# Bulk steps of a state-space scan: products moved from two engines to ScalarE, in a kernel that interleaves the scan with attention

## The chip, the cores and the metric

One core of a Trainium2 chip runs the whole program in one launch. The metric is the device time of that launch in microseconds (us); lower is better. The engines are named as the profile names them: PE is TensorE (matrix products), DVE is VectorE, ACT is ScalarE, POOL is GpSimd and SP is SyncE, which here only issues transfers.

## What is computed

The reference is a two-layer backbone over 1024 latent tokens and 256 context tokens of width 1024, in fp32. Layer 0 runs latent attention (8 heads) and a bidirectional S5 state-space layer side by side; layer 1 is a gated recurrence; each layer ends with a convolutional feed-forward part. Only layer 0's mixer is touched here:

```python
# attention, per head, over context + latent tokens
s = einsum('bqhd,bkhd->bhqk', q, k) * MLA_SCALE
p = softmax(s); att = einsum('bhqk,bkhd->bqhd', p, v)

# S5, 32 groups of 64 complex states, both directions
x = einsum('blgp,gnp->blgn', u, bb)            # re and im
s = associative_scan(s[t] = lb * s[t-1] + x[t])  # complex
y = Re(einsum('blgn,gpn->blgp', s, c)) + d * u  # gelu, gate
z = gelu(y); z = z * sigmoid(z @ w_glu)
out = concat([att, z]) @ w_out
```

## The kernel before

The program is written once as a stream of tile operations. The tile framework orders each engine's instructions when it builds the program, from priorities (the order in which they are written) and its own timeline; on the chip every engine then works through its own list in that fixed order. Where the text speaks of an order, it is this list.

**Attention** (`attention`, from L694). `qk(h)` makes the keys and queries of head h and `attend(h)` uses them, one head behind; `merge` interleaves the steps of `attend(h)`, `qk(h + 1)`, the S5 half-passes and the adaLN products (tile `pada`, L257). All fp32 products of attention are made from rounded high and low parts (`mm3`, L100 to L105: three products; `split`, L108 to L114: a copy to the high part on ACT and a subtraction for the low one). For each block of 512 or 256 queries `attend` goes over 10 (or 2) key tiles: scores in `pS` by `mm3`, the exponential `p` on ACT (L821), its rounded part `ph` on ACT and its rest `pl` on DVE or POOL in turn (L111, L114), and three products into `po` (L826 to L828). The tiles `p`, `ph` and `pl` have two places each.

The softmax needs a maximum per query. `qk` computes rounded scores once more (L793), reduces them on DVE (`mx`, L796, and `mm`, L801 or L803), turns the column of maxima into a row with one fp32 product per 128 queries against the identity (`pm`, L806) and stores the row as row 96 of the queries in high and low parts (L807: the copy on ACT, the subtraction on DVE). Scores then come out with the maximum subtracted.

**S5** (`S5Half.run`, from L867). Twice, for 16 groups each ("half 0" and "half 1"): the inputs `U` are loaded and multiplied into the state tile `H` (`pV`, L889, evicted on ACT at L892), for both directions d. Then comes a scan in three parts over 160 slots of 8 tokens: a bulk pass up over two levels, a sequential scan over every fourth slot on POOL (38 steps of three operations, L931 to L934), and a bulk pass down over two levels. The outputs `pY` (L950, L953) follow, with a gelu on ACT and DVE (L954 to L959), and go to DRAM as `Zd`, from where the gate (`zs`, `pglu`) reads them after attention.

A bulk step is a complex multiply-add on strided slots: two operations. Direction 0 runs on DVE, direction 1 on POOL:

```python
e.tensor_tensor(t, Mh[...].to_broadcast([128, n, 2, 16]), at(src, [[0, 2], [161, 16]]), op=OP.mult)   # L908
for b in range(2):
    e.tensor_tensor(o, o, t[:, :, :, 8 * b:8 * b + 8], op=OP.add)                                     # L912
```

Each product instruction covers up to 16 (DVE) or 20 (POOL) slots. There are four bulk stages in the program: half 0 up, half 0 down, half 1 up, half 1 down. In this text they are stages A, B, C and D. In the trace they lie at about 306 to 343, 404 to 460, 673 to 714 and 795 to 852 us.

Of the kernel before, what the change touches and what calls it, by code (L numbers as in the profile page):

```python
# [11 lines left out]
R = mybir.dt.float32r  # L12
I32 = mybir.dt.int32
AF = mybir.ActivationFunctionType
OP = mybir.AluOpType
# [5 lines left out]
T = SEQ + CTX  # L21
# [672 lines left out]
def attention(k, A):  # L694
    nc = k.nc
    P = Pool(k, "att")
# [4 lines left out]
    for b in range(2):  # L701
        split(nc, KT[b][0][64:96, :], KT[b][1][64:96, :], k.rope[64:96, :], elo="v")
        nc.vector.tensor_copy(KT[b][0][96:97, :], k.ones[96:97, 0:1].to_broadcast([1, T]))
        nc.vector.tensor_copy(KT[b][1][96:97, :], k.zero[96:97, 0:1].to_broadcast([1, T]))
        nc.gpsimd.tensor_copy(Vt[b][0][:, :, 64:128], k.ones[:, 0:1].unsqueeze(1).to_broadcast([128, 10, 64]))
    wkv = A["mla_w_ukv"][0].rearrange("(a p) (h m) -> p a h m", p=128, m=128)
    wuq = A["mla_w_uq"][0].rearrange("(a p) m -> p a m", p=128)
# [1 line left out]
    gk = k.cols[:, k.at["mla_kv_norm", 0]:][:, 0:2]  # L709
    vd = k.tc.dram_tile([T, 512], F, name="vd")  # L710
    S5 = S5Half(k, A)


    vp = Pool(k, "vp")
# [21 lines left out]
    def qk(h):  # L736
# [30 lines left out]
        for s, e in BLK:  # L767
            n = e - s
            ps = bank(k, "pq", "C")
            with behind(k, k.pace):  # L770
                for a in range(3):
                    mm3(nc, ps[:, :n], [w[:, a * 128:a * 128 + 128] for w in wq], [x[a][:, s:e] for x in cq], a == 0, a == 2)
            t = W([128, 512], tag="tq", bufs=2)
            nc.vector.tensor_tensor(t[0:64, :n], ps[64:128, :n], k.rqk[64:128, s:e], op=OP.mult)
            nc.vector.tensor_tensor(t[64:96, :n], ps[0:32, :n], k.rope[0:32, s:e], op=OP.mult)
            if s < SEQ:
                x = W([128, 512], tag="rc")
                nc.vector.tensor_tensor(x[64:96, :n], ps[32:64, :n], k.rope[32:64, s:e], op=OP.mult)
                nc.vector.tensor_tensor(t[64:96, :n], t[64:96, :n], x[64:96, :n], op=OP.add)
            split(nc, q[0][0:96, s:e], q[1][0:96, s:e], t[0:96, :n], elo="v")  # L780
            yield 1

            kb = BLK if s < SEQ else BLK[2:]
            mx = W([128, 4, 3], tag="mx", bufs=2)
            mm_ = W([128, 4], tag="mm", bufs=2)
            nt = n // 128
            jobs = [(j, (i,), ks, ke) for i in range(nt) for j, (ks, ke) in enumerate(kb) if ke < T]
            jobs += [(len(kb) - 1, (i, i + 1), SEQ, T) for i in range(0, nt, 2)]
            for x, (j, tiles, ks, ke) in enumerate(jobs):
                ps = bank(k, "pS", "C")  # L790
                for i, t in enumerate(tiles):
                    with behind(k, k.pace):
                        nc.tensor.matmul(ps[:, i * 256:i * 256 + ke - ks], lhsT=q[0][0:96, s + t * 128:s + t * 128 + 128],  # L793
                                         rhs=kk_[0][0:96, ks:ke], start=True, stop=True)
                t, m = tiles[0], len(tiles)
                nc.vector.tensor_reduce(mx[:, t:t + m, j:j + 1], ps[:].rearrange("p (m x) -> p m x", m=m),  # L796
                                        axis=AX.X, op=OP.max, negate=True)
                if x % 3 == 2 or x == len(jobs) - 1:
                    yield 1
            if len(kb) > 1:  # L800
                nc.vector.tensor_reduce(mm_[:, :nt], mx[:, :nt, :len(kb)], axis=AX.X, op=OP.min)  # L801
            else:
                nc.vector.tensor_copy(mm_[:, :nt], mx[:, :nt, 0])  # L803
            pm = bank(k, "pm", "C")
            for i in range(nt):
                nc.tensor.matmul(pm[96:97, i * 128:i * 128 + 128], lhsT=mm_[:, i:i + 1], rhs=k.ident[:], start=True, stop=True)  # L806
            split(nc, q[0][96:97, s:e], q[1][96:97, s:e], pm[96:97, :n], elo="v")  # L807
            yield 1

    def attend(h):  # L810
        b = h % 2
        q, kk_, v = QT[b], KT[b], Vt[b]
        for s, e in BLK:
            n = e - s
            po = bank(k, "po", "B")
            tiles = list(range(10)) if s < SEQ else [8, 9]
            for i, t in enumerate(tiles):
                ps = bank(k, "pS", "A")
                k.pace = mm3(nc, ps[:, :n], [x[0:97, t * 128:t * 128 + 128] for x in kk_], [x[0:97, s:e] for x in q], True, True)
                p = PP([128, 512], tag="p", bufs=2)  # L820
                nc.scalar.activation(p[:, :n], ps[:, :n], AF.Exp, scale=SCALE)  # L821
                ph = PP([128, 512], R, tag="ph", bufs=2)
                pl = PP([128, 512], R, tag="pl", bufs=2)
                split(nc, ph[:, :n], pl[:, :n], p[:, :n], ehi="a", elo="p" if i % 2 else "v")
                st, sp = i == 0, i == len(tiles) - 1
                nc.tensor.matmul(po[:, :n], lhsT=v[0][:, t], rhs=ph[:, :n], start=st, stop=False)  # L826
                nc.tensor.matmul(po[0:64, :n], lhsT=v[1][:, t], rhs=ph[:, :n], start=False, stop=False, skip_group_check=True)
                nc.tensor.matmul(po[:, :n], lhsT=v[0][:, t], rhs=pl[:, :n], start=False, stop=sp)  # L828
                yield 1


            o = AO([128, 512], tag="ao")
            nc.scalar.activation(o[0:65, :n], po[0:65, :n], AF.Copy)
            nc.sync.dma_start(out=k.attd[64 * h:64 * h + 64, s:e], in_=o[0:64, :n])
            k.last_sum = nc.sync.dma_start(out=k.atts[h:h + 1, s:e], in_=o[64:65, :n])
            yield 1
# [19 lines left out]
class S5Half:  # L856
# [11 lines left out]
    def run(self):  # L868
        k, nc, P = self.k, self.k.nc, self.P
        E = nc.gpsimd  # L870
        for hh in range(2):
# [26 lines left out]
            def bulk(i, up, d):  # L898


                h = 1 << i
                e, tag, m = ((nc.vector, "RO", 16), (E, "Tm", 20))[d]
                src, dst = ((h, 2 * h), (h, 0))[d] if up else ((0, h), (2 * h, h))[d]
                for j in range(0, 80 // h, m):
                    n = min(m, 80 // h - j)
                    t = P([128, m, 2, 16], tag=tag, bufs=2 - d)[:, :n]
                    at = lambda s0, dims: raw(H, s0 + 2 * h * j + 16 * 161 * d, [[2 * h, n]] + dims)
                    e.tensor_tensor(t, Mh[:, i, d].rearrange("p a b q -> p a (b q)").unsqueeze(1)  # L908
                                    .to_broadcast([128, n, 2, 16]), at(src, [[0, 2], [161, 16]]), op=OP.mult)
                    o = at(dst, [[8 * 161, 2], [161, 8]])  # L910
                    for b in range(2):
                        e.tensor_tensor(o, o, t[:, :, :, 8 * b:8 * b + 8], op=OP.add)  # L912
                    yield 1

            def both(levels, up):
# [752 lines left out]
```

## Time and profile before

| what | value |
|---|---|
| median of 3 runs | 3792.78 us (3787.41 to 3795.8) |
| time of the profiled execution | 3789.94 us |
| its span on the core | 3788.1 us |
| mean granted clock of TensorE | 0.966 of full speed |
| busy share of the span: PE, DVE, ACT, POOL | 95%, 55%, 29%, 31% |
| attention and S5 | about 240 to 930 us of the span |

The granted clock is the share of TensorE's full 2.4 GHz that it was given; its two levels are 2.4 and 1.2 GHz. A busy share close to 100% at a clock of 1.00 means that TensorE sets the pace of a stretch; a lower share or a lower clock means that something else does.

### The profile page before, as it was taken

Reading aid. Unit: us, or ns where it says so; the run is one execution under the profiler, and the core shown is the slowest. Engines: PE = TensorE matmul, PEld = TensorE weight load, DVE = VectorE, ACT = ScalarE, POOL = GpSimd, SP = SyncE. Lnnn points to the kernel's source line nnn. Section 1 sums busy time; section 2 is a strip of 40 time slices with the busy share of each in tenths; the row PEclk is TensorE's granted clock in tenths of the full one; section 3 lists DMA queues with packets and bytes.
Section 4 is the critical chain, followed back from the end, with each engine's and each line's share of the span. In section 5 each row is a group of like instructions: output and inputs, shape, how many; then the busy total and the mean of one; then the engine's idle time right before and its main releaser. Section 6 shows DMA issues by size and latency. Waiting matters only on the chain.

```text
span 3788.1 us, 47489 instructions
## 1 busy us (share of the span) xinstructions
PE 3588.2 (95%) x19081; PEld 2910.3 (77%) x19081; DVE 2101.3 (55%) x3294; ACT 1082.7 (29%) x1798; POOL 1178.5 (31%) x1089
## 2 busy tenths in 40 slices
PE   6987899888999999999998999999998999999997
PEld 3764566556788888888887889898987888888885
DVE  7736855784555444444447655565664744545445
ACT  2323445445332121111113322222221511212123
POOL 3627823782442211111114411111122622212122
PEclk9997999988999999999999999999998999999998
DMA  7462345304201111111110210101022111111111
GB/s 243 120 169 73 110 120 141 98 23 146 84 23 34 40 44 40 39 34 34 40 34 29 78 34 29 40 29 40 29 67 89 45 45 45 52 44 51 45 45 45
DMA packets 294301, 243.05 MB, mean 64 GB/s; under 512 B 41214, under 2 KB 255576, under 8 KB 293056
## 3 DMA queue, kind: packets, MB, share of 16 engines
q1 hardware_dynamic: 289152, 227.32, 20.4%
q10 hardware_dynamic: 4928, 12.69, 1.0%
q8 instruction: 150, 2.46, 0.3%
q14 instruction: 71, 0.58, 0.0%
HBM read 203.79 MB, written 38.28 MB: 64 GB/s over the span
## 4 chain that ended last, share of the span: by engine, by line
PE 82%; DVE 7%; POOL 2%; DMA 2%; issue 1%; ACT 1%; SPq 0%; ACTq 0%; POOLq 0%; DVEq 0%
PE pa L105 5%; PE po L103 5%; PE pa L103 5%; PE pa L104 5%; PE po L104 5%; PE po L105 5%; PE pg L103 5%; PE pg L105 5%; PE pg L104 5%; PE ph L104 3%; PE ph L105 3%; PE ph L103 3%; PE pA L1419 3%; PE pmix L103 2%; PE pmix L104 2%; PE pmix L105 2%
## 5 line engine op out<-in xcount | busy, mean ns | idle before, releaser
L114 POOL TENSOR_TENSOR w<-ws,w 128x1024 fp32r<-128x1024 f32 (+1 forms) x205 | 501.1, 2449 | 1570.7 <-ACT w L111 1424.4
L1051 DVE SCALAR_TENSOR_TENSOR acc<-po,mod,acc 128x512 f32<-128x512 f32 (+1 forms) x456 | 309.3, 679 | 559.3 <-PE po L105 559.0
L103 PE MATMUL po<-hh,w 128*128 128x512 f32 (+1 forms) x912 | 342.2, 376 | 11.8 <-DVE acc L1051 10.0
L104 PE MATMUL po<-hl,w 128*128 128x512 f32 (+1 forms) x912 | 335.9, 368 | 5.9 <-DVE hl L114 5.8
L105 PE MATMUL po<-hh,w 128*128 128x512 f32 (+1 forms) x912 | 335.1, 368 | 0.0
L111 ACT ACTIVATE w<-ws 128x1024 fp32r<-128x1024 f32 (+1 forms) x207 | 217.0, 1049 | 409.7 <-PE pg L105 165.3
L103 PE MATMUL pa<-uh,w 128*128 128x512 f32 (+1 forms) x896 | 331.7, 370 | 0.9 <-ACT w L111 0.8
L104 PE MATMUL pa<-ul,w 128*128 128x512 f32 (+1 forms) x896 | 330.2, 369 | 0.1
L105 PE MATMUL pa<-uh,w 128*128 128x512 f32 (+1 forms) x896 | 326.4, 370 | 0.8 <-POOL w L114 0.8
L103 PE MATMUL pg<-uh,w 128*128 128x512 f32 (+1 forms) x872 | 324.2, 372 | 1.9 <-ACT w L111 1.9
L104 PE MATMUL pg<-ul,w 128*128 128x512 f32 (+1 forms) x872 | 322.6, 370 | 0.0
L105 PE MATMUL pg<-uh,w 128*128 128x512 f32 (+1 forms) x872 | 321.5, 372 | 0.6 <-POOL w L114 0.6
L103 PE MATMUL ph<-uh,w 128*128 128x512 f32 (+1 forms) x624 | 238.7, 383 | 1.1 <-ACT uh L1037 1.1
L104 PE MATMUL ph<-ul,w 128*128 128x512 f32 (+1 forms) x624 | 235.1, 377 | 1.5 <-DVE ul L1039 1.5
L105 PE MATMUL ph<-uh,w 128*128 128x512 f32 (+1 forms) x624 | 234.6, 376 | 0.0
L103 PEld LDWEIGHTS po<-hh,w 128*128 128x128 f32 x912 | 173.4, 190 | 46.9 <-DVE acc L1051 12.9
L104 PEld LDWEIGHTS po<-hl,w 128*128 128x128 f32 x912 | 173.9, 191 | 37.9 <-DVE hl L114 6.9
L105 PEld LDWEIGHTS po<-hh,w 128*128 128x128 f32 x912 | 173.8, 191 | 30.2
L103 PEld LDWEIGHTS pa<-uh,w 128*128 128x128 f32 x896 | 168.7, 188 | 32.7 <-ACT w L111 1.0
L105 PEld LDWEIGHTS pa<-uh,w 128*128 128x128 f32 x896 | 168.6, 188 | 32.2 <-POOL w L114 1.3
L104 PEld LDWEIGHTS pa<-ul,w 128*128 128x128 f32 x896 | 168.6, 188 | 32.2 <-DVE ul L1039 0.3
L103 PEld LDWEIGHTS pg<-uh,w 128*128 128x128 f32 x872 | 164.1, 188 | 35.5 <-ACT w L111 2.3
(401 smaller groups left out, 7932.4 us busy)
## 6 DMA issues: line engine op xcount, KB each, us to landing
ws<-in_ffn_w_in_dram SPq DMA_DIRECT2D x88, 512.0 KB
adaw<-in_ada_w_dram SPq DMA_DIRECT2D x80, 512.0 KB
ws<-in_ffn_w_out_dram SPq DMA_DIRECT2D x44, 512.0 KB
ws<-in_hg_w_in_dram SPq DMA_DIRECT2D x40, 512.0 KB
w<-in_ada_w_dram SPq DMA_DIRECT2D x8, 1024.0 KB
ws<-in_ev_w_out_dram SPq DMA_DIRECT2D x10, 512.0 KB
ws<-in_hg_w_out_dram SPq DMA_DIRECT2D x10, 512.0 KB
ws<-in_ev_w_in_dram SPq DMA_DIRECT2D x9, 512.0 KB
```

The lines of the kernel that those rows point to most:

```text
L103: nc.tensor.matmul(ps, lhsT=w[0], rhs=x[0], start=start, stop=False)
L104: nc.tensor.matmul(ps, lhsT=w[0], rhs=x[1], start=False, stop=False)
L105: return nc.tensor.matmul(ps, lhsT=w[1], rhs=x[0], start=False, stop=stop)
L111: nc.scalar.activation(hi, src, AF.Copy)
L114: (nc.gpsimd if elo == "p" else nc.vector).tensor_tensor(lo, src, hi.bitcast(F), op=OP.subtract)
L1051: k.nc.vector.scalar_tensor_tensor(a, ps[:, :e - s], modcol(k, layer, seg, 1 if s >= SEQ else 0, ct), a, op0=OP.mult, op1=OP.add)
L1419: nc.tensor.matmul(ps[:, i * 128:i * 128 + 128], lhsT=km[:, c:c + 128], rhs=raw(Q, c, [[2 * hs, 64 // hs], [SEQ + hs, 2], [1, hs]]), start ...
```

## The change

Three things change.

- The products of a bulk step go to ACT, for both directions. One instruction multiplies one row of H (80 slots at the first level, 40 at the second) with one coefficient per partition, passed as the scale. A stage has 128 of them. The sums stay on DVE (direction 0) and POOL (direction 1), now 640 values each.
- `p` and `ph` get a third place each.
- The row of maxima: `mm` is rounded when it is written and multiplied by a rounded identity in a single-pass product, into partition 0. Only the high part is stored, by one ACT copy. The low part's row is set to zero once for each of the two query tiles.

The new tiles need space. The build shrinks the memory that it sets aside for descriptors made on GpSimd; all queues in the profile are of other kinds.

```diff
+        nc.vector.tensor_copy(QT[b][1][96:97, :], k.zero[96:97, 0:1].to_broadcast([1, T]))
...
+    identr = P([128, 128], R, tag="identr")
+    nc.vector.tensor_copy(identr[:], k.ident[:])
...
-            mm_ = W([128, 4], tag="mm", bufs=2)
+            mm_ = W([128, 4], R, tag="mm", bufs=2)
...
-                nc.tensor.matmul(pm[96:97, i * 128:i * 128 + 128], lhsT=mm_[:, i:i + 1], rhs=k.ident[:], start=True, stop=True)
-            split(nc, q[0][96:97, s:e], q[1][96:97, s:e], pm[96:97, :n], elo="v")
+                nc.tensor.matmul(pm[0:1, i * 128:i * 128 + 128], lhsT=mm_[:, i:i + 1], rhs=identr[:], start=True, stop=True)
+            nc.scalar.activation(q[0][96:97, s:e], pm[0:1, :n], AF.Copy)
...
-                p = PP([128, 512], tag="p", bufs=2)
+                p = PP([128, 512], tag="p", bufs=3)
...
-                ph = PP([128, 512], R, tag="ph", bufs=2)
+                ph = PP([128, 512], R, tag="ph", bufs=3)
...
-                e, tag, m = ((nc.vector, "RO", 16), (E, "Tm", 20))[d]
+                n, m = 80 // h, min(8, 4 * h)
+                e = (nc.vector, E)[d]
                 src, dst = ((h, 2 * h), (h, 0))[d] if up else ((0, h), (2 * h, h))[d]
-                for j in range(0, 80 // h, m):
...
+                for q0 in range(0, 8, m):
...
+                    for b in range(2):
+                        for a in range(2):
+                            for q in range(m):
+                                nc.scalar.activation(t[b][:, a, q], raw(H, 16 * 161 * d + (8 * b + q0 + q) * 161 + src, [[2 * h, n]]),
+                                                     AF.Copy, scale=Mh[:, i, d, a, b, q0 + q:q0 + q + 1])
+                        o = raw(H, 16 * 161 * d + q0 * 161 + dst, [[8 * 161, 2], [161, m], [2 * h, n]])
+                        if b == 0:
+                            yield 1
+                    for b in range(2):
+                        e.tensor_tensor(o, o, t[b], op=OP.add)
                     yield 1
...
-    nc = bacc.Bacc("TRN2", target_bir_lowering=False, num_devices=1)
+    nc = bacc.Bacc("TRN2", target_bir_lowering=False, num_devices=1, dynamic_dma_scratch_size=1024)
```

The change also moves instructions. In the rows below `p<-pS` is an exponential, `ph<-p` its rounded part, `bt<-H,Mh` a bulk product, `po` the sum of p times v, `pY` an S5 output and `pglu` the gate's product.

ACT in the change, stage D, from the last rounded part ahead of it to the first exponential behind it:

```order
L111 ACTIVATE ph<-p 128x512
L916 ACTIVATE bt_5921<-H,Mh 128x40 x16
L916 ACTIVATE bt_5939<-H,Mh 128x40 x16
L916 ACTIVATE bt_5922<-H,Mh 128x40 x16
L916 ACTIVATE bt_5940<-H,Mh 128x40 x16
L811 ACTIVATE QT_2158<-pm 1x512
L111 ACTIVATE ph<-p 128x512
L825 ACTIVATE p<-pS 128x512 x2
L916 ACTIVATE bt_6030<-H,Mh 128x80 x8
L916 ACTIVATE bt_6031<-H,Mh 128x80 x5
L916 ACTIVATE bt_6040<-H,Mh 128x80 x8
```

Before, ACT had none of these products; now 64, and behind two exponentials another 64, stand between attention's instructions in its list.

PE at the end of attention, before:

```order
L826 MATMUL po<-ph,V_2164 128x256
L827 MATMUL po<-ph,V_2165 64x256
L828 MATMUL po<-pl,V_2164 128x256
L950 MATMUL pY<-H,RO 128x160 x4
L953 MATMUL pY<-U,Tm 128x160
```

The last two rows come six times in all, and the first row of `pglu` follows them.

PE where the gate's products begin, in the change:

```order
L103 MATMUL pS<-QT_2160,KT_2156 128x512
L104 MATMUL pS<-QT_2161,KT_2156 128x512
L105 MATMUL pS<-QT_2160,KT_2157 128x512
L103 MATMUL pglu<-zs_8579,w 128x512
L832 MATMUL po<-pl,V_2164 128x512
L103 MATMUL pS<-QT_2160,KT_2156 128x512
L104 MATMUL pS<-QT_2161,KT_2156 128x512
L105 MATMUL pS<-QT_2160,KT_2157 128x512
L104 MATMUL pglu<-zs_8580,w 128x512
```

Before, six S5 outputs and then the gate stood behind attention's last product; now all S5 outputs and the first gate products stand among attention's products, with 49 exponentials (43 of 512 columns) behind stage D.

## Rows read from the trace of the kernel before

**Rows 1.** Chain that ended last, shares of the span by engine

```profile
PE 82%; DVE 7%; POOL 2%; DMA 2%; issue 1%; ACT 1%; SPq 0%; ACTq 0%; POOLq 0%; DVEq 0%
```

**Rows 2.** Busy time by stretch: stretch, length, engines (instructions), TensorE clock, DMA, GB/s

```profile
core 0: us, PE busy (x) PEld busy (x) DVE busy (x) ACT busy (x) POOL busy (x), PEclk, DMA share, GB/s
400.00:460.00 60.00, 50.05 (x242) 30.34 (x241) 51.45 (x72) 24.61 (x44) 53.24 (x70) 0.86 0.33 95
660.00:720.00 60.00, 48.30 (x234) 28.30 (x234) 51.95 (x63) 21.74 (x42) 37.88 (x24) 0.86 0.25 74
780.00:860.00 80.00, 63.82 (x251) 45.37 (x250) 70.89 (x89) 33.15 (x63) 61.10 (x67) 0.84 0.07 19
480.00:590.00 110.00, 110.00 (x597) 73.02 (x598) 63.76 (x112) 56.83 (x123) 26.21 (x27) 1.00 0.52 135
900.00:960.00 60.00, 47.58 (x173) 32.27 (x172) 30.16 (x31) 24.48 (x47) 11.02 (x6) 0.77 0.52 176
```

**Rows 3.** Timeline of stage A: start us, us, engine, instruction, idle before

```profile
306.91 0.42 ACT L892 ACTIVATE H<-pV 128x320 f32<-128x320 f32 x1
...
340.81 0.80 PE L104 MATMUL pS<-QT,KT 97*128 97x512 f32 x1 [11.59 <-DVE QT L114]
...
342.15 1.28 ACT L821 ACT_TABLE_LOAD   x1
343.45 0.60 ACT L821 ACTIVATE p<-pS 128x512 f32<-128x512 f32 x1
```

**Rows 4.** Instructions on tile H: count, ns least/median/most, first and last start

```profile
L912 DVE TENSOR_TENSOR H<-H,RO x64: 377/659/2261, 307.7 to 846.4; 128x256 f32<-128x256 f32 x56, 128x128 f32<-128x128 f32 x8
L912 POOL TENSOR_TENSOR H<-H,Tm x48: 1012/1272/2768, 313.4 to 851.7; 128x320 f32<-128x320 f32 x48
...
L908 DVE TENSOR_TENSOR RO<-Mh,H x32: 615/1136/2807, 306.4 to 837.4; 128x512 f32<-128x512 f32 x28, 128x256 f32<-128x256 f32 x4
L908 POOL TENSOR_TENSOR Tm<-Mh,H x24: 1852/2037/6630, 310.5 to 848.7; 128x640 f32<-128x640 f32 x24
```

**Rows 5.** Costliest groups of ACT by shape: count | busy us, mean ns | idle before

```profile
L111 ACT ACTIVATE ph<-p 128x512 fp32r<-128x512 f32 x160 | 99.3, 629 | 37.5 <-PE po L827 34.1 <-PE po L828 0.5
L821 ACT ACTIVATE p<-pS 128x512 f32<-128x512 f32 x160 | 93.7, 594 | 112.2 <-DVE pl L114 50.1 <-PE pS L105 33.4 <-POOL pl L114 24.8
...
L1037 ACT ACTIVATE uh<-acc,lnm 128x256 fp32r<-128x256 f32 x48 | 25.2, 590 | 14.5 <-DVE acc L1031 14.5
...
L728 ACT ACTIVATE vo<-pv,rkc 128x512 f32<-128x512 f32 x10 | 6.9, 687 | 17.7 <-PE pv L105 9.9 <-DMA vd<-vo 5.9 <-DMA U<-Sd 1.8
...
L111 ACT ACTIVATE wk<-wks 128x128 fp32r<-128x128 f32 x8 | 2.4, 304 | 4.7 <-PE pk L105 4.7
```

**Rows 6.** Timeline of ACT where four of one kind follow each other

```profile
2993.30 2.08 ACT L1037 ACTIVATE uh<-acc,lnm 128x256 fp32r<-128x256 f32 x4 [5.85 <-DVE acc L1031]
```

**Rows 7.** Timeline of PE, two rounded 512-column products at full clock

```profile
350.29 0.40 PE L828 MATMUL po<-pl,V 128*128 128x512 f32 x1
350.53 0.40 PE L103 MATMUL pS<-QT,KT 97*128 97x512 f32 x1
```

**Rows 8.** Timeline of PE at the end of attention

```profile
904.47 0.28 PE L828 MATMUL po<-pl,V 128*128 128x256 f32 x1
...
918.23 2.50 PE L950 MATMUL pY<-H,RO 64*128 64x160 f32 x8 [0.59 <-ACT zt L955]
...
930.25 1.22 PE L103 MATMUL pglu<-zs,w 128*128 128x512 f32 x2 [8.70 <-ACT zs L1205]
```

**Rows 9.** The row of maxima: timeline, then groups by shape, 240 to 960 us

```profile
326.60 1.22 PE L806 MATMUL pm<-ident,mm 128*1 128x128 f32 x8 [0.49 <-DVE mm L801]
...
L806 PE MATMUL pm<-ident,mm 128*1 128x128 f32 x160 | 21.5, 274 | 2.5 <-DVE mm L803 1.3 <-DVE mm L801 1.0
...
L114 DVE TENSOR_TENSOR QT<-pm,QT 1x512 fp32r<-1x512 f32 x16 | 11.2, 697 | 8.8 <-ACT QT L111 8.4
```

**Rows 10.** Exponentials of 512 columns from 855 to 910 us

```profile
L821 ACT ACTIVATE p<-pS 128x512 f32<-128x512 f32 x19 | 11.0, 591 | 4.5 <-DVE pl L114 2.7 <-POOL pl L114 1.5 <-PE pS L105 0.4
```

More of the change, by code (lines that the diff above doesn't have):

```diff
@@ L901, in bulk @@
                 h = 1 << i
-                e, tag, m = ((nc.vector, "RO", 16), (E, "Tm", 20))[d]
+                n, m = 80 // h, min(8, 4 * h)
+                e = (nc.vector, E)[d]
                 src, dst = ((h, 2 * h), (h, 0))[d] if up else ((0, h), (2 * h, h))[d]
-                for j in range(0, 80 // h, m):
[L905 to L910, printed above, removed]
-                    for b in range(2):
-                        e.tensor_tensor(o, o, t[:, :, :, 8 * b:8 * b + 8], op=OP.add)
+                for q0 in range(0, 8, m):
+                    t = [P([128, 2, 4, 80], tag=f"bt{b}", bufs=2).rearrange("p a q x -> p (a q x)")[:, :2 * m * n]
+                         .rearrange("p (a q x) -> p a q x", a=2, q=m) for b in range(2)]
+                    for b in range(2):
+                        for a in range(2):
[7 more added lines that the diff above has]
+                        e.tensor_tensor(o, o, t[b], op=OP.add)
                     yield 1
```

## Prediction

> **What bounds the kernel now.** I read the chain that ended last first, because it says which engine to argue about. TensorE holds 82% of it [rows 1]. An edit on other engines therefore pays only where TensorE waits for them, or runs at a low clock after having waited. So I next took the busy time by stretch and looked for slices where TensorE is neither full nor at clock 1.00. While the first half's outputs run, it is busy 110.00 of 110 us at clock 1.00: nothing can be gained there [rows 2]. In the stretches around bulk stages B, C and D and at the end of attention it is busy 50.05 of 60, 48.30 of 60, 63.82 of 80 and 47.58 of 60 us, at clocks of 0.86, 0.86, 0.84 and 0.77 [rows 2]. I call length minus busy time times clock the loss of a stretch; it is a rough figure, since the clock is a mean. That gives 60 - 43.0 = 17.0, 60 - 41.5 = 18.5, 80 - 53.6 = 26.4 and 60 - 36.6 = 23.4 us. DVE is busy 70.89 of 80 us around stage D, and ACT only 33.15 [rows 2]: the work leaves a full engine for one with room.
>
> Two places need the timeline. In stage A TensorE stands idle for 11.59 us until DVE has written the low part of the row of maxima, and the first exponential starts at 343.45 us [rows 3]. At the end of attention its last product starts at 904.47 us; then come S5 outputs alone, and the gate's first product waits 8.70 us and starts at 930.25 us [rows 8].
>
> **The price of a product on ACT.** None of this shape is in the trace. A copy of 128 columns takes 304 ns and one of 512 takes 629 [rows 5], 0.846 ns per column, so 80 columns take 263 and 40 take 230 ns. A scale read per partition is dearer: 687 ns for the copy with such a scale against 594 for an exponential of the same shape [rows 5], 93 ns more. Instructions in a row overlap: four of 590 ns [rows 5] span 2.08 us [rows 6], so they start (2.08 - 0.59) / 3 = 0.497 us apart, 0.093 sooner than they end. The two cancel: 0.263 us per product of 80 columns and 0.230 per product of 40. Bounds: with neither overlap nor cheaper pointer 0.356 and 0.323; with the pointer hidden as well 0.170 and 0.137. I take the middle, since rows 6 show the overlap on an instruction that has two such operands. A stage of 64 + 64 products costs ACT 16.8 + 14.7 = 31.5 us.
>
> **What is removed.** From DVE 32 products with a median of 1.136 us, from POOL 24 with one of 2.037 [rows 4]: about 36 and 49 us. The sums stay: 24 of 640 values on each engine, against 64 and 48 smaller ones now. DVE takes 0.659 us for 256 values or fewer, POOL 1.272 for 320 [rows 4], so a sum of 640 is about 1.6 and 2.5 us; a stage's six on POOL make 15 us, half of ACT's 31.5, and run beside it. The new limit of a stage is ACT.
>
> **Stage A: -10 us.** The last eviction of H starts at 306.91 us [rows 3]. In the change's list 24 products of 80 and 64 of 40 columns follow it ahead of the first exponential (the other 40 columns of 80 stand earlier, between evictions, while transfers hold that phase up): 6.3 + 14.7 = 21.0 us. Three copies and one of weights, about 2.1, and the 1.28 us table load [rows 3] add 3.4, and I allow 1.5 for waits: 307.2 + 25.9 = 333 against 343.45.
>
> **Stages B, C and D: -5 us.** Exponentials stand in the same list, so the products now hold attention up. From the list I count what ACT and TensorE have to do from the first to the last product of a stage, TensorE at one 512-column product per 0.24 us [rows 7]. B: 31.5 us of products and 28 other instructions at about 0.5 make 45.5 us, beside 32 us of TensorE's work: 13.5 lost. C has 96 products left (the first 32 stand between evictions): 23.1 + 4 = 27 beside 14, 13 lost. D: 31.5 + 3.5 = 35 beside 14, 21 lost. Each also costs about 3 us of low clock afterwards; behind the idle 11.59 us of rows 3 products take 0.80 us and not the 0.40 of rows 7. That is 47.5 + 9 = 56.5 against 17.0 + 18.5 + 26.4 = 61.9. So the three stages change hardly at all: the wait only moves from DVE to ACT.
>
> **End of attention: -18 us.** This is the largest term, and it comes from the order. Before, 19 exponentials of 512 columns start after 855 us, when stage D has ended [rows 10]; in the change 43 of that size stand behind it, so all outputs and the first gate products are covered by attention's products. Of the 23.4 us lost there I leave 5, for the sums of the last head, which must go to DRAM and back, and for two more table loads on ACT (2 x 1.28 us [rows 3]), since the gate's function now runs between exponentials. In the row a load takes 1.28 us and the exponential behind it starts 0.02 us after its end. The Trainium skill (ScalarE: Activation LUTs, What ACT_TABLE_LOAD costs) adds a drain of about 1.38 us to each switch of tables; by it, as an estimate, two switches cost 5.3 and not 2.6 us, and the sum would be 2.7 us higher. No such drain stands in the rows.
>
> **The row of maxima: -8 us.** Eight passes span 1.22 us and one takes 0.274 [rows 9], so they start 0.135 us apart; 160 make 21.6 us. Half as many remain, at 0.135 us (as one pass now) or at a quarter of the 0.24 us of rows 7, 0.06: 10.8 or 4.8 us. That saves 11 to 17 us of TensorE, of which I count 60% of the middle, since only full stretches count. The 24 subtractions on DVE (0.697 us at 512 [rows 9]) also go; the 11.59 us behind one of them are in stage A's sum. One copy of 128 columns and two rows of zeros at the start are hidden by a phase that waits for transfers; without that cover they would cost 3 us.
>
> **Third places: 0.** Exponentials waited 50.1 us for a low part on DVE and 24.8 for one on POOL [rows 5], mostly inside the stages counted above. Elsewhere TensorE is full. Bounds: 5 us gained, none lost.
>
> **Sum:** -10 - 5 - 18 - 8 = -41 us against the profiled execution's 3789.94: 3749. The median shown is 2.8 us above that execution, so the forecast for a median is **3750 us**, rounded between 3749 and 3752. Behind the gate TensorE's list is almost unchanged, so what is won stays won.
>
> **Rivals.**
>
> *The queue of ACT is the new bottleneck (slower).* 440 products (88 + 128 + 96 + 128) stand where an exponential waits behind them. Each 0.093 us more on one of them costs 41 us, the whole gain; so it decides from a mean price of 0.34 us. Without overlap the price is 0.34, and the result 3790. If ACT then also waits for the sums that free its two places, with POOL's sum at twice its most, 5.5 us instead of 2.5 [rows 4], about two more waits of 3 us per stage add 24: 3815. For it: blocks of 64 with no exponential between in stage D. Against it: rows 6. Chance 0.10.
>
> *The sums still limit the stages.* DVE and POOL slow each other down: sums take 0.377 (128 values) to 2.261 us on DVE, and 1.012 to 2.768 for one shape on POOL [rows 4]. Six POOL sums at 5.5 us are 33 us, as long as ACT's products, and the last two of each level stand at its end. Three more waits of 4 us give 3762. The Trainium skill (GPSIMD Engine Reference, 1. Specifications) says that GpSimd shares its SBUF interfaces with VectorE and contends with instructions that have two SBUF inputs; by that rule the sums, which all have two, go on contending after the change, and the spread in rows 4 agrees. Chance 0.12.
>
> *The end of attention is not covered.* If stages B to D run so late on the chip that outputs reach TensorE's list late, or the last head's sums hold the gate up, the 18 us do not come: 3768. For it: the order rests on the framework's own durations. Against it: 43 exponentials with six products of 0.24 us each are 62 us of cover. Chance 0.13.
>
> *Third places and freer DVE and POOL gain more*, as low parts come sooner in all of attention: 3730. Chance 0.05.
>
> **How the numbers follow.** The forecast has 0.60, the rivals 0.10, 0.12, 0.13 and 0.05. The range goes from 3724, where products cost 0.15 us and ACT no longer holds B to D (25 us less), to 3786, which takes in the second and third rival together (3780) and leaves most of the first out. A measurement of this kernel can tell 0.2%, 7.6 us, from no change. Faster by more: the forecast, the last three rivals and little else, 0.88; within it, a part of the first rival, 0.04; slower, the rest of it, 0.08.
>
> **What would show it.** Products on ACT of about 0.35 us each in the groups, starting 0.23 to 0.26 us apart; the first exponential near 333 us; ACT busy without a gap in B, C and D with TensorE idle for some 10 us in C and 20 in D; gate products before attention's last one, and no idle 8.70 us. Products that start 0.34 us apart, or TensorE idle for over 30 us in D, or a gate that begins as late after attention as now, would make it wrong.

## Result and the profile after

The changed kernel takes 3752.2 us (median of 4 runs, 3742.72 to 3754.69) where the kernel before takes 3793.85 (3787.41 to 3795.8): ratio 0.9884, 95% interval 0.9872 to 0.9897. The forecast was 3750. Ratios and intervals here and below compare fast runs alone; one of the nine runs of `places_alone`, at a mean clock of 0.648, took 5007.28 us and is left out of its ratio. The profiled execution took 3752.72 us, with a span of 3750.9.

The page's busy times and its chain of waits, after:

```profile
PE 3562.0 (95%) x19001; PEld 2899.7 (77%) x19001; DVE 2008.3 (54%) x3201; ACT 1210.6 (32%) x2312; POOL 1086.1 (29%) x1041
...
PE 82%; ACT 4%; DVE 3%; POOL 3%; DMA 2%; issue 1%; SPq 0%; ACTq 0%; POOLq 0%; DVEq 0%
```

TensorE still holds 82% of the chain [rows 1]; ACT now has 4% of it, more than DVE. Next, ACT's timeline in stage A after (start us, us, instruction, count, idle before):

```profile
306.35 0.42 ACT L896 ACTIVATE H<-pV 128x320 f32<-128x320 f32 x1
...
310.35 15.75 ACT L916 ACTIVATE bt<-H,Mh 128x80 f32<-128x80 f32 x61
326.12 0.58 ACT L811 ACTIVATE QT<-pm 1x512 fp32r<-1x512 f32 x1
...
329.58 2.65 ACT L916 ACTIVATE bt<-H,Mh 128x40 f32<-128x40 f32 x10
332.25 1.28 ACT L825 ACT_TABLE_LOAD   x1
333.54 1.08 ACT L825 ACTIVATE p<-pS 128x512 f32<-128x512 f32 x2
```

The first exponential starts at 333.54 us, against 343.45 in [rows 3] and 333 in the prediction, and products fill ACT ahead of it (the 61 in one row are of both shapes). The groups by shape (busy us, mean ns of one | idle before):

```profile
L916 ACT ACTIVATE bt<-H,Mh 128x80 f32<-128x80 f32 x256 | 69.5, 354 | 1.9 <-DVE H L922 1.5
L916 ACT ACTIVATE bt<-H,Mh 128x40 f32<-128x40 f32 x256 | 67.3, 354 | 1.7 <-POOL H L944 1.6
L922 POOL TENSOR_TENSOR H<-H,bt 128x640 f32<-128x640 f32 x24 | 40.9, 1703 | 66.2 <-ACT bt L916 64.4 <-ACT H L896 1.4
L922 DVE TENSOR_TENSOR H<-H,bt 128x640 f32<-128x640 f32 x24 | 25.4, 1059 | 27.8 <-ACT bt L916 27.4
L810 PE MATMUL pm<-identr,mm 128*1 128x128 f32 x80 | 9.4, 227 | 0.0
```

A product takes 0.354 us at 80 and at 40 columns. The sums are cheaper than forecast (1.70 on POOL and 1.06 on DVE, against 2.5 and 1.6) and wait for products (27.4 of the 27.8 us that DVE stood idle before them): the limit of a stage is ACT, as predicted. What that does to TensorE, by stretch (columns as in [rows 2]; stages B, C, D and the end of attention):

```profile
420.00:480.00 60.00, 53.99 (x260) 35.35 (x260) 42.67 (x66) 49.79 (x153) 24.57 (x26) 0.89 0.29 85
640.00:700.00 60.00, 43.62 (x215) 26.67 (x214) 30.04 (x45) 46.07 (x136) 40.78 (x65) 0.80 0.25 77
740.00:800.00 60.00, 40.62 (x172) 26.75 (x171) 29.02 (x43) 46.93 (x159) 17.61 (x14) 0.72 0.14 40
860.00:940.00 80.00, 75.70 (x304) 52.97 (x303) 51.47 (x56) 55.75 (x91) 28.43 (x19) 0.96 0.53 169
```

Length minus busy time times clock gives losses of 11.9, 25.1, 30.8 and 7.3 us, where the prediction had 17.0, 18.5, 26.4 and 23.4 before. In these stretches B got better, C and D worse, and the end of attention gave 16 of its 23 us back; since the stretches moved with the stages (D has 80 us before and 60 here, the end 60 and 80), this is a rough comparison, and a closed account stands further down. TensorE's waits between 640 and 860 us name the cause in C and D (total us, times, longest), and ACT's timeline of D shows what stood ahead:

```profile
PE pS L797 <- ACT QT L111: 14.9, 2, 14.6
PE pY L960 <- DVE H L922: 9.8, 2, 6.6
PE po L830 <- ACT ph L111: 6.3, 1, 6.3
```

```profile
741.31 16.43 ACT L916 ACTIVATE bt<-H,Mh 128x40 f32<-128x40 f32 x64 [1.25 <-POOL H L944]
757.76 0.58 ACT L811 ACTIVATE QT<-pm 1x512 fp32r<-1x512 f32 x1
758.37 0.63 ACT L111 ACTIVATE ph<-p 128x512 fp32r<-128x512 f32 x1
758.91 1.06 ACT L825 ACTIVATE p<-pS 128x512 f32<-128x512 f32 x2
759.86 16.50 ACT L916 ACTIVATE bt<-H,Mh 128x80 f32<-128x80 f32 x64
```

In C a query tile's rounding stands in ACT's queue behind products, and in D an exponential's rounded part. The second wait lies in D too, and it is the longer one there: S5 outputs wait on TensorE for the last sums on DVE, and those sums waited for products on ACT.

### The profile page after: what moved, and what is told of

Its sections match the earlier page's. It is cut to its first block, busy times and chain, and to the rows that moved or that the text cites. A ratio compares the mean times of both kernels' runs of the same rounds, so it can differ in the third digit from the quotient of the medians.

```text
span 3750.9 us, 47623 instructions
## 1 busy us (share of the span) xinstructions
PE 3562.0 (95%) x19001; PEld 2899.7 (77%) x19001; DVE 2008.3 (54%) x3201; ACT 1210.6 (32%) x2312; POOL 1086.1 (29%) x1041
## 4 chain that ended last, share of the span: by engine, by line
PE 82%; ACT 4%; DVE 3%; POOL 3%; DMA 2%; issue 1%; SPq 0%; ACTq 0%; POOLq 0%; DVEq 0%
PE pa L105 5%; PE pa L103 5%; PE pa L104 5%; PE po L103 5%; PE pg L103 5%; PE pg L105 5%; PE pg L104 5%; PE po L104 5%; PE po L105 5%; PE ph L104 3%; PE ph L105 3%; PE ph L103 3%; PE pA L1429 3%; ACT bt L916 3%; PE pmix L103 2%; PE pmix L104 2%
## 5 line engine op out<-in xcount | busy, mean ns | idle before, releaser
L1114 ACT ACTIVATE a<-pa 128x512 f32<-128x512 f32 (+1 forms) x112 | 61.3, 547 | 431.6 <-PE pa L105 430.5
```

The lines of the kernel that those rows point to most:

```text
L1114: nc.scalar.activation(at[t][:, col(o):col(o) + e - o], ps[:, o - s:e - s], AF.Copy)
```

## Experiments

### The parts one by one

Each of the three parts was put alone into the kernel before, and each was undone alone in the changed kernel. The edits are those of the diff ahead of the prediction, taken or left whole. For instance `no_products` puts this back:

```diff
-                n, m = 80 // h, min(8, 4 * h)
-                e = (nc.vector, E)[d]
+                e, tag, m = ((nc.vector, "RO", 16), (E, "Tm", 20))[d]
...
-                for q0 in range(0, 8, m):
...
+                for j in range(0, 80 // h, m):
```

`maxima_alone` and `no_maxima` differ from their base in the row of maxima:

```diff
-            mm_ = W([128, 4], tag="mm", bufs=2)
+            mm_ = W([128, 4], R, tag="mm", bufs=2)
...
-            split(nc, q[0][96:97, s:e], q[1][96:97, s:e], pm[96:97, :n], elo="v")
+            nc.scalar.activation(q[0][96:97, s:e], pm[0:1, :n], AF.Copy)
```

and the `places` kernels in two numbers. All of these kernels are built with the smaller descriptor memory of the change, and no run tests that by itself.

```diff
-                p = PP([128, 512], tag="p", bufs=2)
+                p = PP([128, 512], tag="p", bufs=3)
...
-                ph = PP([128, 512], R, tag="ph", bufs=2)
+                ph = PP([128, 512], R, tag="ph", bufs=3)
```

Expected of `maxima_alone`:

> The kernel before with the single-pass row of maxima alone (and the two rows that it needs at the start); products as before, two places. Sum on record: 8 us less TensorE time that counts, so 0.2% under the kernel before; first exponential still near 343 us, since DVE's products hold that stage. Theory from the two profiles: about 14 us, because 17 us of TensorE's time are gone and nearly all of attention is full, so 0.4% under. Rival: stage A's 10 us belong to this part as well, since what the first exponential waited for was the low part of this row, behind DVE's products: then it starts near 331 us and the kernel is 0.6 to 0.7% (24 us) under.

Of `products_alone`:

> The kernel before with the products on ACT alone, exact row of maxima, two places. Sum on record: stage A 10, stages B to D 5, end of attention 18, so 33 us under the kernel before. Theory from the two profiles: A 10, B to D 3 the other way, end of attention 16, so 23 us under, 0.6%. Rival (without a third place the exponentials cannot run ahead of a block of products): under 10 us gained.

Of `places_alone`:

> The kernel before with the third places alone; products on DVE and POOL, exact row of maxima. Sum on record: 0, at most 5 us gained. With the products on ACT the places gave 0.6 us the wrong way and 5 us the right way, inside the intervals; with the products on DVE and POOL two kernels that differ in the places lie 10 us apart (ratios 0.9956 and 0.9990). Theory (two chains: the scan sets the end of attention there, so exponentials that run ahead change nothing): ratio 0.999 to 1.001. Rival (low parts that come late behind DVE's products are what the third place covers): 0.996 to 0.998.

Of `no_maxima`:

> The changed kernel with the row of maxima in exact products and with its low part on DVE, as before. Sum on record: 8 us over the changed kernel. Theory from the two profiles: 14 us over it, 3766, with the first exponential at most 3 us later than 333, since DVE is free of products there. Rival (the row's wait is worth more than its passes): over 20 us, because the copy on ACT and then DVE's subtraction stand behind products again.

Of `no_products`:

> The changed kernel with the products on DVE and POOL as before; single-pass row and three places stay. Sum on record: 33 us over the changed kernel, 3785. Theory from the two profiles: 23 us over it, 3775, first exponential near 343. Rival (stage A belongs to the row of maxima): 13 us over it, 3765, first exponential near 331.

Of `no_places`:

> The changed kernel with two places for p and for its rounded part. Sum on record: 0. The two kernels with products on ACT that differ in nothing but the places and the row lie 0.6 us apart with the row's 8 us still to come, so theory: within 3 us of 3752. Rival (third places do gain, up to 5 us by the sum's bound, and as the kernels with products on DVE suggest, 3780 against 3790, up to 10): 3757 to 3762.

Measured (median us, ratio with its interval to the runs of the kernel before that were taken with it, whose medians lie between 3790.6 and 3794.12; the last columns are starts from the profiled execution: the first and the last exponential, the last S5 output product, the first mean of the layer norm, which needs attention, outputs and gate):

| kernel | median | ratio | interval | first exp | last exp | last output | first mean |
|---|---|---|---|---|---|---|---|
| before | 3793.85 | 1 | | 343.4 | 902.0 | 921.1 | 1023.0 |
| maxima_alone | 3790.32 | 0.9990 | 0.9979 to 1.0001 | 321.2 | 872.2 | 917.5 | 1017.9 |
| places_alone | 3784.05 | 0.9978 | 0.9965 to 0.9990 | 340.7 | 894.8 | 912.7 | 1013.3 |
| products_alone | 3759.67 | 0.9910 | 0.9895 to 0.9924 | 333.3 | 909.9 | 872.4 | 996.6 |
| no_products | 3779.96 | 0.9956 | 0.9938 to 0.9974 | 323.7 | 872.9 | 915.9 | 1020.9 |
| no_places | 3757.09 | 0.9894 | 0.9877 to 0.9912 | 331.0 | 909.4 | 863.3 | 995.1 |
| no_maxima | 3760.29 | 0.9909 | 0.9895 to 0.9924 | 332.1 | 902.3 | 868.4 | 991.8 |
| after | 3752.2 | 0.9884 | 0.9872 to 0.9897 | 333.5 | 903.5 | 864.3 | 988.7 |

The products alone are worth 33 us, which is what the prediction's three terms for them add up to (10 + 5 + 18); my reading from the two profiles, 23, missed. Undone in the changed kernel they are worth 28 us (3779.96 - 3752.2), between that reading and the sum. The row of maxima is worth 6 us (`products_alone` against `no_places`, 0.9910 and 0.9894) to 9.5 us (`no_maxima` against the changed kernel, 0.9909 and 0.9884) once the products are moved, 4 alone, where no change lies just inside the interval. The intervals of both pairs overlap, so its size is not settled, nor that it is worth more beside the moved products. The third places are worth nothing to 5 us beside the moved products, and 8 us alone (0.9978, clear of no change). `no_products` and `maxima_alone`, which differ in the places alone, lie 10 us apart in the medians, with intervals apart; their profiled executions lie the other way (3784.54 and 3779.73 us), so the traces can't show where these 10 us come from.

The surprise is `maxima_alone`: its first exponential starts 22 us sooner. The wait for the row's low part, which in [rows 3] stood behind DVE's products, is gone. The maxima themselves still stand among those products, but their row comes 8 us sooner (318.26 us, against 326.60 in [rows 9]). Yet the kernel gains 4 us. The rows on the two ends show why. Before (first and last start in the fourth column):

```profile
L821 ACT ACTIVATE p<-pS x176: 361/597/602, 343.4 to 902.0; 128x512 f32<-128x512 f32 x160, 128x256 f32<-128x256 f32 x16
...
L953 PE MATMUL pY<-U,Tm x64: 297/300/633, 483.9 to 921.1; 128*128 128x160 f32 x64
...
L1011 PE MATMUL pmean<-lns,onesd x56: 377/591/628, 1023.0 to 3718.6; 128*128 128x512 f32 x40, 128*128 128x256 f32 x16
```

`maxima_alone`, with the first row of maxima, and its gate's wait from the list of TensorE's waits:

```profile
318.26 0.58 PE L810 MATMUL pm<-identr,mm 128*1 128x128 f32 x4 [3.03 <-DVE mm L805]
...
L825 ACT ACTIVATE p<-pS x176: 364/597/602, 321.2 to 872.2; 128x512 f32<-128x512 f32 x160, 128x256 f32<-128x256 f32 x16
...
L957 PE MATMUL pY<-U,Tm x64: 297/403/635, 489.9 to 917.5; 128*128 128x160 f32 x64
...
PE pglu L103 <- ACT zs L1209: 8.7, 1, 8.7
```

After:

```profile
L825 ACT ACTIVATE p<-pS x176: 364/597/625, 333.5 to 903.5; 128x512 f32<-128x512 f32 x160, 128x256 f32<-128x256 f32 x16
...
L963 PE MATMUL pY<-U,Tm x64: 297/352/634, 462.5 to 864.3; 128*128 128x160 f32 x64
...
L1021 PE MATMUL pmean<-lns,onesd x56: 377/591/697, 988.7 to 3682.4; 128*128 128x512 f32 x40, 128*128 128x256 f32 x16
```

Two chains end this phase: attention (last exponential) and the S5 scan with its outputs (last `pY`). Before, the scan ends last, 19 us behind attention. `maxima_alone` ends attention 30 us sooner and the scan 4 us sooner, and the mean follows the scan. In all four kernels of the table with products on DVE and POOL, the first mean starts 100.4 to 105.0 us after the last output (1023.0 - 921.1 = 101.9 before). In the four with products on ACT the scan ends 34 to 46 us ahead of attention, and the mean starts 85.2 to 89.5 us after the last exponential. The whole change ends the scan 57 us sooner (921.1 to 864.3) and leaves attention's end where it was (902.0 and 903.5): most of what is won there is the outputs and the gate, which now run under attention. The products by themselves pull the two chains apart: between `no_products` and the changed kernel the scan ends 52 us sooner and attention 31 us later (872.9 to 903.5), with its instructions behind products in ACT's queue.

### The price of a product

```diff
+                            src0 = 16 * 161 * d + (8 * b + q0) * 161 + src
                             for q in range(m):
-                                nc.scalar.activation(t[b][:, a, q], raw(H, 16 * 161 * d + (8 * b + q0 + q) * 161 + src, [[2 * h, n]]),
-                                                     AF.Copy, scale=Mh[:, i, d, a, b, q0 + q:q0 + q + 1])
+                                sc = Mh[:, i, d, a, b, q0 + q:q0 + q + 1]
+                                if (d, i) == (0, 0):
+                                    if q % 2 == 0:
+                                        nc.scalar.activation(t[b][:, a, q:q + 2], raw(H, src0 + q * 161, [[161, 2], [2 * h, n]]), AF.Copy, scale=sc)
+                                elif (d, i) == (1, 1):
+                                    for x in (0, 20):
+                                        nc.scalar.activation(t[b][:, a, q, x:x + 20], raw(H, src0 + q * 161 + 2 * h * x, [[2 * h, 20]]), AF.Copy, scale=sc)
+                                else:
+                                    nc.scalar.activation(t[b][:, a, q], raw(H, src0 + q * 161, [[2 * h, n]]), AF.Copy, scale=0.5)
```

> The changed kernel with four forms of product on ACT. In direction 0 a product of the first level takes 160 columns with one scale per partition (two rows of slots, half as many instructions), and one of the second level 40 columns with a constant scale; in direction 1 the first level takes 80 columns with a constant scale, and the second 20 columns with a scale per partition (twice as many instructions). The scales of the first three are not those of the reference, so the values differ; the time of a product does not hang on them. Theory on record: 0.263 us apart at 80 columns, 0.230 at 40, 0.846 ns per column and 0.093 us for the scale: 0.33 at 160, 0.137 at 40 and 0.170 at 80 with a constant, 0.21 at 20. Theory from the changed kernel's rows (354 ns and 0.257 us apart for 80 and 40 alike): a floor, so 0.25 at 20 as well, and 0.25 or a little less at 40 and 80 with a constant; only the 160 columns lie above it, at 0.32.

Its timeline of ACT, from its one execution (start us, us, instruction, count):

```profile
753.23 7.12 ACT L923 ACTIVATE bt<-H,Mh 128x20 f32<-128x20 f32 x32
760.25 2.71 ACT L925 ACTIVATE bt<-H 128x40 f32<-128x40 f32 x16
...
769.86 2.72 ACT L920 ACTIVATE bt<-H,Mh 128x160 f32<-128x160 f32 x8
...
775.01 2.75 ACT L925 ACTIVATE bt<-H 128x80 f32<-128x80 f32 x16
```

and the durations (least/median/most ns):

```profile
L925 ACT ACTIVATE bt<-H x256: 253/262/307, 267.9 to 784.1; 128x80 f32<-128x80 f32 x64, 128x40 f32<-128x40 f32 x64
L923 ACT ACTIVATE bt<-H,Mh x256: 310/317/357, 311.5 to 769.6; 128x20 f32<-128x20 f32 x128
L920 ACT ACTIVATE bt<-H,Mh x64: 421/429/461, 267.2 to 780.0; 128x160 f32<-128x160 f32 x64
```

A span less one duration, over one instruction less, gives the time apart: 0.219 us at 20 columns, (7.12 - 0.317) / 31; 0.327 at 160; with a constant scale 0.163 at 40 and 0.166 at 80. The changed kernel's 61 in a row, of 80 and 40 columns with a scale per partition, give 0.257, (15.75 - 0.354) / 60; in D its 64 of 40 give 0.255 and its 64 of 80 give 0.256. So both theories missed in part, the prediction's at 40 columns alone (0.230 and, with a constant, 0.137). A scale per partition costs 0.09 us, as the prediction had it. There is no floor at 0.257, since 20 columns come cheaper. First-level products read every second word of H, second-level ones every fourth: from 80 to 160 columns at a stride of 2 words a column costs (0.327 - 0.257) / 80 = 0.88 ns, and from 20 to 40 at a stride of 4 words (0.257 - 0.219) / 20 = 1.9 ns. So a column costs about double at the wider stride, and 40 there cost what 80 cost here. Each slope rests on two points; that both lines come to nearly the same time at no columns, 0.187 us (0.257 - 80 x 0.00088) and 0.181 us (0.219 - 20 x 0.0019), speaks for it.

### What is left of the loss

If products in ACT's queue cost C and D their 25 and 31 us, it should help to let attention's instructions past them, or to put fewer there. Five kernels tried it. `products_last` gives each product a rank 2000 places later in the scheduler's order; `last_c` and `last_d` do so in stage C or D alone:

```diff
-                                nc.scalar.activation(t[b][:, a, q], raw(H, 16 * 161 * d + (8 * b + q0 + q) * 161 + src, [[2 * h, n]]),
-                                                     AF.Copy, scale=Mh[:, i, d, a, b, q0 + q:q0 + q + 1])
+                                with k.tc.high_priority(offset=-2000):
+                                    nc.scalar.activation(t[b][:, a, q], raw(H, 16 * 161 * d + (8 * b + q0 + q) * 161 + src, [[2 * h, n]]),
+                                                         AF.Copy, scale=Mh[:, i, d, a, b, q0 + q:q0 + q + 1])
```

with `-2000 if hh and up else 0` in `last_c`, `-2000 if hh and not up else 0` in `last_d`. `dir1_act` keeps the code of before, under the name `bulk_old`, for direction 0 (`dir1_act_last`: with rank -3000 besides):

```diff
-                g = [chain(*(bulk(i, up, d) for i in levels)) for d in range(2)]
+                g = [chain(*((bulk if d == 1 else bulk_old)(i, up, d) for i in levels)) for d in range(2)]
```

> The changed kernel with the products ranked 2000 places later in the scheduler's order, so that exponentials and roundings go ahead of them on ACT: in stage D 14 exponentials stand between the products and not 2, and no block is longer than 16. Theory: what the changed kernel still loses in C and D (23 and 30 us by busy time and clock) is ACT's queue; then these two fall to about 10 each, some 30 us, while the scan of slots ends later by the 39 us that it now has to spare, so 10 to 30 us under the changed kernel. Rival (the scan's own length sets the end of attention): the outputs end behind attention again, the loss returns there, and the time is within 5 us of the changed kernel or above it.

> The changed kernel with the products of direction 1 (POOL's before) on ACT and those of direction 0 on DVE as before: ACT's share of a stage is 16.5 us and not 33, and both engines work at once. Theory (ACT's queue in C and D is what is left): each of B, C, D loses 6 to 10 us less, so 10 to 25 us under the changed kernel. Rival (DVE's products hold low parts and splits up as before, so the wait only moves back): within 5 us of it, or above.

> As the kernel with direction 1 on ACT, and those products ranked 3000 places later: no block of products without an exponential is longer than 19, and 18 exponentials stand behind the last output. Theory: both gains, so 20 to 40 us under the changed kernel. Rival (DVE's share now limits): as the kernel without the ranking, within 5 us.

> The changed kernel with the products of stage D alone ranked 2000 places later (14 exponentials among them, no block over 18). With all stages so ranked, busy time and clock put D's loss at 22 us and not 40, C's at 26 and not 35, and the stretch from 800 to 940 us at 47 and not 21, because the scan's last output came at 878 us while attention ended at 857. Theory (two chains, and the longer one sets the end): with D alone the last output comes near 875 and attention ends near 885, so nearly all of D's 18 us come: 3733 to 3740. Rival (the scan sets the end as soon as D is stretched): 3745 to 3752.

> The changed kernel with the products of stage C alone ranked 2000 places later (in stage C eight more exponentials stand among them, and no block is over 24; stage D has a block of 128). Theory: C's 9 us come, attention still ends behind the scan, so 3740 to 3746; the last output moves from 864 to about 875 us. Rival (D's longer block takes back what C gives): 3749 to 3756.

| kernel | median | ratio | interval | last exp | last output | first mean |
|---|---|---|---|---|---|---|
| products_last | 3743.06 | 0.9867 | 0.9852 to 0.9882 | 857.8 | 878.4 | 978.8 |
| dir1_act | 3746.6 | 0.9879 | 0.9864 to 0.9894 | 898.4 | 851.6 | 984.8 |
| dir1_act_last | 3751.21 | 0.9880 | 0.9863 to 0.9898 | 894.8 | 854.4 | 982.6 |
| last_d | 3733.4 | 0.9842 | 0.9824 to 0.9860 | 874.5 | 867.7 | 970.9 |
| last_c | 3728.18 | 0.9836 | 0.9820 to 0.9851 | 870.9 | 857.7 | 962.5 |

`products_last` by the same four stretches:

```profile
420.00:480.00 60.00, 54.66 (x290) 34.16 (x288) 44.22 (x69) 51.28 (x152) 30.87 (x33) 0.97 0.37 103
640.00:700.00 60.00, 54.26 (x302) 33.63 (x301) 45.20 (x62) 51.87 (x152) 29.13 (x28) 0.94 0.39 115
740.00:800.00 60.00, 53.89 (x212) 37.38 (x210) 42.26 (x64) 50.60 (x147) 33.78 (x52) 0.86 0.03 6
860.00:940.00 80.00, 68.69 (x249) 47.21 (x248) 47.23 (x53) 34.89 (x62) 18.68 (x13) 0.81 0.43 143
```

Its losses are 7.0, 9.0, 13.7 and 24.4: C and D fall by 16 and 17 us, so the theory on ACT's queue holds, and the end of attention takes 17 back. The scan ends last again, 21 us behind attention, the gate waits 8.9 us, and the mean starts 100.4 us after the last output, as in the kernels with products on DVE and POOL. So its rival holds as well, in part, and the gain is 9 us by the medians, with intervals that overlap. Stretching one stage only leaves the two chains 7 us (`last_d`) and 13 us (`last_c`) apart, and these two are the fastest kernels of the study, `last_c` 24 us under the changed kernel by the medians, 18 by the ratios, and clear of its interval: `last_d` came out at the low end of what was expected, `last_c` 12 us below it. In `last_c`:

```profile
640.00:700.00 60.00, 54.63 (x306) 35.03 (x305) 41.20 (x60) 47.11 (x123) 38.78 (x63) 0.97 0.37 109
740.00:800.00 60.00, 37.95 (x151) 26.49 (x151) 29.56 (x39) 50.15 (x166) 20.09 (x14) 0.74 0.06 15
860.00:940.00 80.00, 76.25 (x318) 54.50 (x317) 52.66 (x61) 44.97 (x74) 30.81 (x21) 0.98 0.49 162
```

The last input of stage C and its last products on ACT, first in `last_c`, then in the changed kernel:

```profile
633.19 0.44 ACT L896 ACTIVATE H<-pV 128x320 f32<-128x320 f32 x1
...
664.87 1.14 ACT L917 ACTIVATE bt<-H,Mh 128x40 f32<-128x40 f32 x4
```

```profile
647.41 0.41 ACT L896 ACTIVATE H<-pV 128x320 f32<-128x320 f32 x1
...
653.01 16.39 ACT L916 ACTIVATE bt<-H,Mh 128x40 f32<-128x40 f32 x64
```

Stage C loses 7.0 us instead of 25.1, D 31.9 (30.8 in the changed kernel), and the end of attention 5.3. The last output does not come later but 6.6 us sooner than in the changed kernel. The rank moved more than the products: the stage's last input is evicted 14 us sooner, so that its last product, though exponentials stand in between, ends at 666.0 us against 669.4, and the scan pays no price. Why C's gain is 18 us, where I expected 9, stays open. `dir1_act` and `dir1_act_last` lie within the changed kernel's interval. In `dir1_act` TensorE waits 16.3 us in all for low parts on POOL and 9.0 us once for a sum on DVE behind its products, so, much as its rival had it, the wait moves to other engines.

## Why the prediction was right

*The sum was right, and the products' share; how that share is made up is in part luck.* Products 33 forecast, measured 33 alone and 28 undone; row of maxima 8, measured 4 to 9.5 with intervals that overlap; third places 0, at most 5, measured 0 to 5 beside the moved products. The products were forecast as three terms, 10, 5 and 18, so their split can be looked at as well. In slices of 20 us from 240 us to the first mean, losses and TensorE's work (busy time times clock) make up the whole time, so nothing falls between stretches (us, from the profiled executions; sums within 0.1):

| kernel | loss to 340 | loss 340 to 860 | loss 860 to mean | loss in all | work |
|---|---|---|---|---|---|
| before | 51.8 | 72.1 | 24.2 | 148.2 | 634.8 |
| products_alone | 45.3 | 64.1 | 14.1 | 123.6 | 633.0 |
| maxima_alone | 43.6 | 78.0 | 38.9 | 160.4 | 617.5 |
| no_products | 43.3 | 78.6 | 40.3 | 162.2 | 618.7 |
| after | 47.6 | 74.9 | 8.3 | 130.8 | 617.9 |

The products by themselves give 6.5, 8.0 and 10.1 us, and undone -4.3, 3.7 and 32.0: both times most at the end of attention, but no term has a size of its own apart from what else is in the kernel.

*Stage A, -10: right in the time, wrong in what it is worth by itself.* The first exponential came at 333.54 us for a forecast of 333. But `maxima_alone` brings it to 321.2 and gains 4 us. The prediction added this term as if every microsecond won there lasted to the end. As I read it, it lasts only where the scan no longer ends last, which the products bring about, and the row of maxima does not; no run moves the first exponential and nothing else. Once the row is single-pass, the products make the first exponential later, 323.7 us in `no_products` against 333.5.

*Stages B to D, -5: right for the products, with the low clock sized too small.* By the stretches shown with the result it is 67.8 us against 61.9 before, so 6 us worse, where 56.5 was forecast. That pair has the row of maxima in it, which alone adds 5.9 us of loss from 340 to 860 us; the products by themselves take 8.0 off there, and 3.7 undone. The idle time was sized well: 60 minus busy time gives 6.0, 16.4 and 19.4 us, 41.8 in all for a forecast of 47.5. The low clock was not: busy time times (1 - clock) gives 5.9, 8.7 and 11.4 us, 26 in all, and the prediction allowed 3 for each stage. The rows of before could have told it: the same product there gives 7.0, 6.8 and 10.2 us [rows 2].

*End of attention, -18: right for the whole change, and its cause too.* It is 16 us by the same stretches, from 23.4 to 7.3, and 15.9 from 860 us to the first mean. The gate's first product starts at 876.0 us, ahead of the last exponential at 903.5, and the wait of 8.70 us [rows 8] is gone. What the prediction did not say is that this term is the hinge for the others.

*The row of maxima, -8: at the lower of its two prices, and the share that counts not shown.* TensorE is busy with it for 9.4 us against 21.5 [rows 9]. In its timeline four in a row span 0.40 us:

```profile
322.01 0.40 PE L810 MATMUL pm<-identr,mm 128*1 128x128 f32 x4
```

One takes 0.22, so they start (0.40 - 0.22) / 3 = 0.06 us apart, the lower price. Of the work saved the prediction counted 60%. In `maxima_alone` the work falls by 17 us, but the losses rise by 12, and the first mean starts 5 us sooner; between `no_maxima` and the changed kernel it starts 3 us sooner.

*Third places, 0: right beside the moved products only.* In the kernel before they give 8 us, over the bound of 5. There the scan's last output comes 8.4 us sooner with them; why the scan gains from places of p was not tried.

*Where the rest of the 33 lies.* In the profiled executions `products_alone` is 26.4 us ahead at the first mean (24.6 of loss and 1.8 of work) and 31.2 at the end. The 4.8 us between lie behind the part that was changed; over the 14 profiled executions of this text that part takes 2757.8 to 2767.7 us, in no order of the edits. So a few us of each figure here may be scatter, and so may the step from 31 in one execution to 33 in the medians.

*The rivals.* ACT's queue is the new limit of a stage, but its price did not reach the 0.34 us from which it would have decided: 0.257. ACT's two places cost nothing that shows: in the groups above products waited 1.9 and 1.7 us in all. The sums limit no stage: POOL's took 1.70 us and not 5.5, and where TensorE waited 9.8 us for sums, they had waited for products. Their spread stays, on DVE for one shape (least, median and most ns):

```profile
L922 DVE TENSOR_TENSOR H<-H,bt x24: 807/842/1808, 302.8 to 774.3; 128x640 f32<-128x640 f32 x24
```

The Trainium skill (GPSIMD Engine Reference, 1. Specifications) has GpSimd share its SBUF interfaces with VectorE and contend with instructions that have two SBUF inputs. The spread agrees with that rule, but no run tests its cause. The end of attention is covered. The Trainium skill (ScalarE: Activation LUTs, What ACT_TABLE_LOAD costs) adds a drain of about 1.38 us to a switch of tables. No such gap stands on either side of the load in stage A: it starts 0.02 us after the last product's end (329.58 + 2.65 = 332.23), and the exponential 0.01 us after its own, at 333.54.

## What to carry to other kernels

Where two chains of work share an engine and meet at one point, first find which of them ends last: work won on the other is lost at the meeting point. In `maxima_alone` attention ended 30 us sooner and the kernel gained 4. Moving work to an engine with room shortens the chain that it belongs to and puts a queue in front of the other; so see the rank of the moved instructions as part of the move, and try to stretch the chain that has time to spare until both end close together. And price idle time of TensorE with the low clock behind it, read from the stretches themselves: here, in three stretches, it came to six tenths of the idle time.

## What the runs showed of the hardware

On ACT a column read from SBUF cost 0.88 ns at a stride of 2 words and 1.9 ns at 4, so products of 80 and of 40 columns both took 0.354 us. The Trainium skill (ScalarE: Activation LUTs, What ACT_TABLE_LOAD costs) gives 186 ns, 0.833 ns per column and 93 ns per operand that is a pointer, with an overlap of 93 ns. By it, as an estimate, 80 columns take 346 ns and 40 take 312. It agrees with 354 at the narrow stride and not at the wide one, where the measurement decides.
